# Three pairs of conditioning columns leave the first layer's attention steps

## The chip, the cores and the metric

One Trainium2 chip, of which the kernel uses one core. The metric is device time in microseconds for one execution. Before the change three runs took 1669.55, 1670.0 and 1672.5 us; their median, 1670.0 us, is the time before.

## The reference

Two encoder layers over 512 tokens of width 1024. With `c_act = silu(c)`, each layer computes its conditioning, mixes tokens, normalises, sends tokens through experts and normalises again:

```python
mod = c_act @ ada_w[i] + ada_b[i]                 # 6 * 1024 columns
sh1, sc1, g1, sh2, sc2, g2 = jnp.split(mod, 6)
h = x * (1 + sc1) + sh1
y = neighbourhood_mixer(h) if i == 0 else gqa_mixer(h)
x = layer_norm(ALPHA * x + (1 + g1) * y)
h = x * (1 + sc2) + sh2
y = hierarchical_moe(h)                           # 4 groups, 32 experts, top 2
x = layer_norm(ALPHA * x + (1 + g2) * y)
```

Everything is float32. So the six conditioning vectors of a layer are wanted at different times: `sh1, sc1` at its entry, `g1` after the mixer, `sh2, sc2` at the routing, `g2` in the experts. Each vector is two blocks of 512 columns, called (layer, block): blocks 0 and 1 are `sh1`, 2 and 3 `sc1`, 4 and 5 `g1`, 6 and 7 `sh2`, 8 and 9 `sc2`, 10 and 11 `g2`.

## The kernel before

**Conditioning.** A block needs 2 MB of weights, which come as two loads of 1 MB, (`ada`, layer, block, half). Blocks 0 to 3 of layer one are made at the very start. Seven others (`ADAV`) are accumulated on DVE, two multiply-adds in a step. Twelve (`ADAP`: six pairs and one single block) are made on PE by `adap`, in the steps of layer one's attention that `ADAP` names: for each block and half four matmuls, each with a 128x32 stationary operand (a shifted window of `Z`, which holds `c_act` in one column) and 512 moving columns, in four column groups of the array; a record of the trace is half of such a matmul, so a pair has 32. They add up in one PSUM tile, and a DVE add puts the sum into `mod[l]`, the SBUF tile in which every block has its row. `row` and `ada_cols` read it: `row` spreads a block over the partitions, `ada_cols` turns blocks into columns by four thin matmuls and one DVE operation for each vector.

**Layer one's attention** (`mixer0`, `neighbours`, `flow`) is 32 steps (16 heads in pairs, four blocks of queries). A step computes scores on PE, subtracts the maximum and adds the bias on DVE, exponentiates on ACT, turns the result on PE, copies it on ACT and multiplies by the values on PE. Between these, `flow` puts a fixed number of projection matmuls for later steps (`STREAM`, `RATE`), which last until about step 26. PE and DVE run in the order that is written here (`manual_schedule`).

**Layer one's output projection and routing** (`layer`, the block for `l == 0`): for each of four tiles of 128 tokens the projection (`sums`), the transposes (`turnX`), the router's logits, and two tiles later the `router`, a chain of small DVE operations with one PE step in the middle. PE's order is written out here as well. The last tile's transposes and logits follow behind that block, then `moe`, whose `begin` gathers the first experts' tokens while DVE routes the last tile.

**The experts** (`moe`): 32 experts by twos, 12 loads of 1 MB for each two, PE's order written out. At the end eight `unit`s close the sum over experts and DVE and ACT normalise (`scales`, `finish`). Then comes `overflow`, a block behind a branch that all engines take together.

**Layer two's mixer** (`mixer1`): it splits the key and value weights on ACT, DVE and POOL, turns X into eight transposed blocks on PE (PSUM tile `pt`, two buffers), scales them on ACT and DVE, and projects them; then four query projections, then `router_weights(1)`, which folds `sc2, sh2` into the router's weights. Here the order on all engines but SP is a planner's: it takes the earliest written instruction that its own estimate says is ready.

**Loads.** `plan` lists all weights in the order of their use; `W` hands one out, returns its slot to a list of free ones and issues the next loads of the list into free slots. All are issued by SP, in order, and each waits until its slot's last reader has finished, so one that waits holds up all behind it. Attention has 5 slots of 1 MB for such weights; the experts have 14 (5 of `w0`, 3 of `wy`, 2 of `no`, 4 of `nh`). Weights of layer two can only go into the 5 until layer two begins. In the stage of the output projection the list offers three `wy`, one `w0` and two `no`; the others are added behind it.

## Time and profile before

| | us |
|---|---|
| median of three runs | 1670.0 |
| profiled execution | 1673.3 |
| its span | 1671.6 |
| PE busy | 1574.7 (94%) |
| DVE busy | 700.6 (42%) |
| ACT busy | 437.6 (26%) |
| POOL busy | 162.3 (10%) |

The rows below come from that one execution. Times are us from the span's start unless marked ns. PE is the matrix engine, DVE the vector, ACT the scalar, POOL the general engine; SP issues the loads. A row of the timeline gives start, length, engine, line, operation, output and input tiles, shapes, the count of merged records, and in brackets how long the engine stood idle before it and what released it. Records overlap, so the length of a group is not its share of the engine: the pace is read from start to start.

### The profile page before, as it was taken

How to read it: one execution, taken by the hardware profiler on the slowest of the kernel's cores; microseconds unless marked ns; L12 is line 12 of the kernel's file. 1: busy time of each engine (PE TensorE's matmuls, PEld its weight loads, DVE VectorE, ACT ScalarE, POOL GpSimd, SP SyncE). 2: the span in 40 equal slices, each digit the busy share in tenths (PEclk: the TensorE clock that was granted, in tenths of full speed). 3: DMA queues.
4: the chain of work that ended last, by engine and by line, in shares of the span. 5: the costliest groups of instructions: out<-in, count | busy, mean ns of one | idle time of the engine just before them, and what ended most of it. 6: DMA issues, size and time to landing. Idle time of an engine off the chain costs nothing. (4 is left out here: it accounts for less than half of the span.)

```text
span 1671.6 us, 21362 instructions
## 1 busy us (share of the span) xinstructions
PE 1574.7 (94%) x8490; PEld 906.6 (54%) x8490; DVE 700.6 (42%) x1605; ACT 437.6 (26%) x934; POOL 162.3 (10%) x99
## 2 busy tenths in 40 slices
PE   7899997989999999999979989998999999999995
PEld 4676664773544545455448866766354545545442
DVE  3434545574232322323256865666432232323235
ACT  2343335231110111111134475453011111101112
POOL 2322212010000000000014250011000000000001
PEclk9999997999999999999989989999999999999997
DMA  9587872357999999999932000035899999999981
GB/s 328 196 309 269 331 306 104 137 202 295 417 419 420 419 419 420 419 419 420 420 125 102 26 1 25 1 125 206 368 416 420 420 420 420 419 420 420 419 332 51
DMA packets 76198, 493.17 MB, mean 295 GB/s; under 512 B 9876, under 2 KB 11284, under 8 KB 18876
## 3 DMA queue, kind: packets, MB, share of 16 engines
q1 hardware_dynamic: 71916, 485.05, 71.4%
q10 hardware_dynamic: 4176, 6.69, 1.2%
q8 instruction: 69, 1.13, 0.3%
q14 instruction: 37, 0.30, 0.1%
HBM read 489.61 MB, written 2.10 MB: 294 GB/s over the span
## 5 line engine op out<-in xcount | busy, mean ns | idle before, releaser
L300 PE MATMUL gu<-w,xT 128*64 128x512 f32 x2048 | 445.0, 592 | 0.0
L300 PEld LDWEIGHTS gu<-w,xT 128*64 128x64 f32 x2048 | 146.8, 137 | 291.6 <-issue 287.0
L300 PE MATMUL pd<-w,hx 128*64 128x512 f32 x1024 | 228.0, 598 | 0.0
L1391 DVE TENSOR_TENSOR h<-h,gu 128x512 f32<-128x512 f32 x32 | 22.0, 688 | 370.4 <-PE gu L300 370.4
L300 PEld LDWEIGHTS pd<-w,hx 128*64 128x64 f32 x1024 | 70.9, 137 | 140.3 <-issue 136.7
L300 PE MATMUL gc<-OH,zH 128*128 128x256 f32 x480 | 121.5, 291 | 2.6 <-DVE OH L1276 2.6
L300 PE MATMUL gc<-OH,zL 128*128 128x256 f32 x480 | 118.6, 284 | 0.0
L300 PE MATMUL gc<-YH,OT 128*128 128x512 f32 x244 | 104.2, 427 | 1.0 <-DVE X L1358 1.0
L1358 DVE TENSOR_TENSOR X<-X,gc 128x512 f32<-128x512 f32 x128 | 87.4, 688 | 39.3 <-PE gc L300 39.3
L300 PEld LDWEIGHTS gc<-OH,zH 128*128 128x128 f32 x480 | 92.5, 193 | 14.9 <-issue 11.4
L300 PE MATMUL gc<-YL,OT 128*128 128x512 f32 x244 | 96.3, 394 | 0.0
L300 PEld LDWEIGHTS gc<-OH,zL 128*128 128x128 f32 x480 | 92.6, 193 | 0.0
L300 PE MATMUL pw<-w,oH 128*128 128x512 f32 x256 | 86.3, 408 | 0.0
L1414 ACT ACTIVATE YH<-h 128x512 fp32r<-128x512 f32 x32 | 20.2, 630 | 233.6 <-DVE h L1413 233.6
L300 PE MATMUL pj<-wh,hTH 128*128 128x256 f32 (+1 forms) x272 | 71.2, 304 | 9.1 <-ACT hTH L419 4.0
L1294 ACT ACTIVATE xT<-gc,A 128x256 f32<-128x256 f32 x60 | 33.8, 566 | 173.9 <-PE gc L300 173.9
L300 PE MATMUL pj<-wl,hTH 128*128 128x256 f32 (+1 forms) x272 | 68.0, 292 | 0.0
L300 PE MATMUL pj<-wh,hTL 128*128 128x256 f32 (+1 forms) x272 | 65.6, 293 | 0.8 <-DVE hTL L427 0.8
L300 PEld LDWEIGHTS gc<-YH,OT 128*128 128x128 f32 x244 | 45.8, 188 | 37.3 <-DVE X L1358 15.8
L1292 DVE TENSOR_SCALAR xT<-gc,A 128x256 f32<-128x256 f32 x60 | 32.5, 545 | 76.9 <-ACT xT L1294 76.5
L1390 ACT ACTIVATE h<-gu 128x512 f32<-128x512 f32 x32 | 19.1, 597 | 173.0 <-PE gu L300 173.0
L303 PE MATMUL pt<-c_ident,pr 128*128 128x128 f32 x384 | 59.5, 283 | 2.1 <-ACT pr L862 2.0
(345 smaller groups left out, 2355.9 us busy)
## 6 DMA issues: line engine op xcount, KB each, us to landing
w<-in_gu SPq DMA_DIRECT2D x256, 1024.0 KB, 14.3
w<-in_dn SPq DMA_DIRECT2D x128, 1024.0 KB, 13.5
w<-in_ada SPq DMA_DIRECT2D x40, 1024.0 KB, 7.9
wq<-in_wqk SPq DMA_DIRECT2D x16, 512.0 KB, 3.6
w<-in_wo SPq DMA_DIRECT2D x8, 1024.0 KB, 5.8
w<-in_adaq SPq DMA_DIRECT2D x6, 1024.0 KB, 12.0
bias<-in_nab ACTq DMA_DIRECT2D x24, 256.0 KB, 3.4
w<-in_wq SPq DMA_DIRECT2D x4, 1024.0 KB, 4.9
```

What stands on the lines that cost most here:

```text
L300: return self.nc.tensor.matmul(out, l, r, start=start, stop=stop, **kw)
L303: self.nc.tensor.transpose(out, in_, self.ident)
L1292: nc.vector.tensor_scalar(xT[q][:, k, :], ps, s, b, op0=OP.mult, op1=OP.add)
L1294: nc.scalar.activation(xT[q][:, k, :], ps, AF.Identity, scale=s, bias=b)
L1358: nc.vector.tensor_tensor(X[t][:, c], X[t][:, c], ps, op=OP.add)
L1390: nc.scalar.activation(h, gu[0], AF.Silu)
L1391: nc.vector.tensor_tensor(h, h, gu[1], op=OP.mult)
L1414: nc.scalar.activation(YH[j][:, c], y, AF.Copy)
```

## The change

Of `ADAP`'s pairs, three go elsewhere. (0,10),(0,11), the gate `g2` of layer one (`ADAO`), is made at the end of the routing block of layer one, behind `router(NT - 2)`, in the PSUM tile `pw`; its four loads stand in the list ahead of the first expert weights. (1,6),(1,7), `sh2` of layer two (`ADAL[0]`), is made behind the last `unit` of layer one's experts, ahead of `scales` and `finish`; (1,8),(1,9), `sc2` of layer two (`ADAL[1]`), in `mixer1` behind the split of the first weights and ahead of the transposes. Their loads stand ahead of `kv` 0 and `kv` 1. The rest of `ADAP` moves from steps 4, 12, 23, 26 to 5, 11, 19, 26. The columns for `sc2` and `sh2` of layer two, which were made with those for `sc1` and `sh1` in the routing block of layer one, are made by a second `ada_cols` ahead of `router_weights(1)`.

```diff
--- before.py
+++ after.py
@@ -44,8 +44,8 @@
 QPOST = 2
 NWQ = 4
 ADAV = [(0, 6), (0, 7), (0, 8), (0, 9), (1, 0), (1, 1), (1, 2)]
-ADAP = {4: [(0, 4), (0, 5)], 8: [(0, 10), (0, 11)], 12: [(1, 4), (1, 5)], 15: [(1, 6), (1, 7)], 19: [(1, 8), (1, 9)],
-        23: [(1, 10), (1, 11)], 26: [(1, 3)]}
+ADAP = {5: [(0, 4), (0, 5)], 11: [(1, 4), (1, 5)], 19: [(1, 10), (1, 11)], 26: [(1, 3)]}
+ADAO, ADAL = [(0, 10), (0, 11)], [[(1, 6), (1, 7)], [(1, 8), (1, 9)]]
 STREAM = [("qk", 1, 0)] + [("qk", n, i) for i in (1, 2) for n in range(2)] + [("vq", 0)] \
     + [("qk", n, i) for i in (3, 4, 5, 6) for n in range(2)] + [("vq", 1)] + [("qk", n, 7) for n in range(2)]
 RATE = (18, 15)
@@ -133,6 +133,9 @@
         for l in range(DEPTH):
             if l:
                 for c in range(2):
+                    for z in ADAL[c]:
+                        for h in range(2):
+                            add(("ada", *z, h), a["ada"][z[0], z[1], h])
                     add(("kv", c), a["wkv1"][c])
                 for c in range(4):
                     add(("q1", c), a["wq1"][c])
@@ -142,6 +145,8 @@
             for h in range(2):
                 for kh in range(2):
                     add(("wl", l, h, kh), None)
+            if l == 0:
+                ada(0, *(j for _, j in ADAO))
             for j in range(E // 2):
                 for n in range(2):
                     for kh in range(2):
@@ -359,6 +364,18 @@
             nc.vector.tensor_scalar(dst[:, n].rearrange("p (j i) -> p j i", j=2),
                                     pc[:, :, j:j + 2].rearrange("p i j -> p j i"), one, None, op0=OP.add)
 
+    def ada_pair(self, pp, pair, tag):
+        l = pair[0][0]
+        ps = pp.tile([P, F], F32, name=tag, bufs=2)
+        for i, (_, j) in enumerate(pair):
+            for h in range(2):
+                w = self.W(("ada", l, j, h)).rearrange("p (k n) -> p k n", k=4)
+                for k in range(4):
+                    r = 32 * k
+                    self.mm(ps[r:r + 32], self.Z[:, 4 * h + k, 12 - j:44 - j], w[:, k, :], i == 0 and h == 0,
+                            i == len(pair) - 1 and h == 1, tile_position=(0, r))
+        self.nc.vector.tensor_tensor(self.mod[l], self.mod[l], ps, op=OP.add)
+
     def row(self, ps, l, j):
         return self.mm(ps, bcast(self.indc[:, j:j + 1], [P, P]), self.mod[l], True, True)
 
@@ -687,16 +704,7 @@
                 nc.vector.scalar_tensor_tensor(acc, w, s, acc, op0=OP.mult, op1=OP.add)
 
         def adap(pair):
-            l = pair[0][0]
-            ps = pp.tile([P, F], F32, name="pt")
-            for i, (_, j) in enumerate(pair):
-                for h in range(2):
-                    w = self.W(("ada", l, j, h)).rearrange("p (k n) -> p k n", k=4)
-                    for k in range(4):
-                        r = 32 * k
-                        self.mm(ps[r:r + 32], self.Z[:, 4 * h + k, 12 - j:44 - j], w[:, k, :], i == 0 and h == 0, i == len(pair) - 1 and h == 1,
-                                tile_position=(0, r))
-            nc.vector.tensor_tensor(self.mod[l], self.mod[l], ps, op=OP.add)
+            self.ada_pair(pp, pair, "pt")
 
         def aside(n):
             i, b = n // 4, n % 4
@@ -734,6 +742,7 @@
             self.fold_cols(c1[:, 0], c1[:, 1], self.lnc[:, 0, 2], self.lnc[:, 0, 3], self.col[1][:, 0], self.col[1][:, 1])
             w = self.W(("kv", 0))
             whl = [self.split(pool, w[:, 1024 * x:1024 * x + 1024], [P, 1024], 4, (nc.vector, None)[x]) for x in range(2)]
+            self.ada_pair(pp, ADAL[1], "pt")
             acc = [pp.tile([P, 4, HD], F32, name="pj", bufs=4) for t in range(NT)]
             for k in range(KD):
                 self.put_hT(k, self.transp(k, pp, "pt"), hH, hL, c1[:, 0], c1[:, 1], pool, k >= KACT)
@@ -841,6 +850,7 @@
                     if t == QPOST:
                         post()
                 post = lambda c=c, qq=qq, ss=ss: queries(c, qq, ss)
+            self.ada_cols(pp, self.mod[1], self.col[1], ((2, 8, 1.0), (3, 6, 0.0)), "pt")
             self.router_weights(1, pp)
             post()
 
@@ -1035,13 +1045,14 @@
                         if t:
                             hx = turnX(t - 1)
                         if t == NT - 1:
-                            self.ada_cols(pp, self.mod[1], self.col[1], ((0, 2, 1.0), (1, 0, 0.0), (2, 8, 1.0), (3, 6, 0.0)), "pt")
+                            self.ada_cols(pp, self.mod[1], self.col[1], ((0, 2, 1.0), (1, 0, 0.0)), "pt")
                         it = sums(t, 1)
                         run(it, 10)
                         if t:
                             logits(t - 1, lg[:, t - 1, :], hx)
                         run(it, 99)
                     self.router(NT - 2, wk, pp, "pt", lg[:, NT - 2, :], rt)
+                    self.ada_pair(pp, ADAO, "pw")
             else:
                 for t in range(NT):
                     oTs.append([wk.tile([P, KD, P], F32R, name=n, bufs=2) for n in ("oH", "oL")])
@@ -1490,6 +1501,8 @@
             seed(range(NSEED[0], 8))
             for n in range(8):
                 unit(n)
+            if l == 0:
+                self.ada_pair(pp, ADAL[0], "gc")
             self.scales(pool, rt, 0, NT)
             self.finish(l, units, acc, rt)
         self.overflow(l, zH, zL, G2, rt, OH)
```

## Rows read from the trace of the kernel before

**Rows 1.** The page: busy time by engine; DMA issues of one weight, us to landing.

```profile
PE 1574.7 (94%) x8490; PEld 906.6 (54%) x8490; DVE 700.6 (42%) x1605; ACT 437.6 (26%) x934; POOL 162.3 (10%) x99
...
w<-in_wq SPq DMA_DIRECT2D x4, 1024.0 KB, 4.9
```

**Rows 2.** Stretches: busy us (instructions) of each engine, granted clock, DMA share, GB/s.

```profile
95.00:258.00 163.00, 157.02 (x1046) 106.99 (x1044) 75.72 (x178) 60.31 (x151) 29.64 (x13) 0.98 0.78 297
...
360.20:367.00 6.80, 6.79 (x32) 6.80 (x33) 4.27 (x26) 2.88 (x6) 0.00 (x0) 0.50 0.58 245
...
395.00:405.00 10.00, 7.01 (x14) 2.04 (x14) 8.61 (x15) 0.00 (x0) 0.00 (x0) 0.66 0.70 291
...
405.00:415.00 10.00, 10.00 (x50) 3.24 (x48) 5.28 (x16) 1.26 (x2) 0.00 (x0) 1.00 0.68 272
...
800.00:810.00 10.00, 10.00 (x47) 4.00 (x44) 1.14 (x2) 0.60 (x1) 0.00 (x0) 1.00 1.01 419
...
861.50:867.80 6.30, 0.12 (x1) 0.00 (x0) 5.44 (x19) 4.92 (x10) 0.00 (x0) 0.81 0.00 1
...
867.80:879.00 11.20, 8.03 (x36) 7.66 (x37) 5.49 (x11) 7.35 (x9) 6.63 (x6) 0.50 0.16 41
```

**Rows 3.** PE in order of time, layer one's attention: start, us, instruction, idle before.

```profile
158.25 3.64 PE L300 MATMUL pt<-w,Z 128*32 128x512 f32 x32
...
161.83 0.66 PE L300 MATMUL po<-pts,V 128*64 128x128 f32 x8
...
177.75 2.78 PE L300 MATMUL pt<-w,Z 128*32 128x512 f32 x24
...
182.48 1.76 PE L300 MATMUL pt<-w,Z 128*32 128x512 f32 x8 [1.95 <-DMA w<-in_ada]
...
184.17 1.12 PE L300 MATMUL po<-pts,V 128*64 128x128 f32 x8
...
233.78 0.69 PE L300 MATMUL pj<-hTH,wh 128*128 128x512 f32 x1 [2.46 <-ACT V L479]
```

**Rows 4.** Tile pt in attention: ns of one, min/median/max.

```profile
L699 DVE TENSOR_TENSOR mod<-mod,pt x6: 686/689/690, 103.0 to 242.5; 128x512 f32<-128x512 f32 x6
...
L300 PE MATMUL pt<-c_indc,mod x8: 185/266/266, 226.2 to 226.9; 128*128 128x20 f32 x8
```

**Rows 5.** PE in order of time, layer one's last routing.

```profile
359.43 0.30 PE L303 MATMUL pt<-c_ident,X 128*128 128x128 f32 x1 [3.46 <-DVE Mb L1126]
...
360.21 3.63 PE L300 MATMUL pt<-c_wr,hx 128*128 128x36 f32 x16
...
372.27 0.36 PE L300 MATMUL gc<-OH,zH 128*128 128x256 f32 x1 [1.02 <-DVE OH L1276]
```

**Rows 6.** DVE in order of time, same stretch.

```profile
363.87 0.25 DVE L971 SCALAR_TENSOR_TENSOR lg3x<-cs,nm,pt 128x36 f32<-128x36 f32 x1 [2.22 <-PE pt L300]
...
371.70 0.42 DVE L1276 TENSOR_TENSOR OH<-c_iota,posx 128x256 fp32r<-128x256 f32 x1
```

**Rows 7.** SP's DMA issues: three moments, start, us, count.

```profile
289.39 2.01 SPq L272 DMA_DIRECT2D w<-in_gu  x4
...
850.86 3.76 SPq L272 DMA_DIRECT2D w<-in_wq  x2
...
877.85 0.34 SPq L272 DMA_DIRECT2D w<-in_wq  x1
```

**Rows 8.** PE in order of time, end of layer one and entry of layer two.

```profile
823.57 13.90 PE L300 MATMUL gu<-w,xT 128*64 128x512 f32 x64
...
867.85 1.94 PE L303 MATMUL pt<-c_ident,X 128*128 128x128 f32 x8 [6.23 <-ACTq L1169]
...
872.91 0.58 PE L300 MATMUL pj<-wh,hTH 128*128 128x256 f32 x1 [3.12 <-ACT hTH L419]
```

**Rows 9.** Weights' landing, issues of 800 to 808 us.

```profile
DMA to landing us min/median/max: 18.0/20.0/20.5
```

## The prediction

> **What bounds the kernel now.** I read the page's busy times first: PE is busy 94% of the span [rows 1], so the question of each stage is whether work on PE there stands alone or beside a wait. Then I cut the span into stages. In layer one's attention PE works 157.02 of 163.00 us at a granted clock of 0.98, while DVE has 75.72 and ACT 60.31 [rows 2]. The three pairs leave from there, and a matmul that goes there should give back nearly its own time. Then I read PE in order of time at the four places that receive something. At the last routing of layer one PE stands 3.46 us for DVE and afterwards works at half clock (0.50 from 360.2 to 367.0) [rows 2, 5]. At the end of layer one it stands 6.23 us at the branch ahead of the overflow block while DVE is busy 5.44 of 6.30 us [rows 2, 8]. At the entry of layer two it transposes, stands 3.12 us for ACT, and works at half clock until 879 [rows 2, 8]. In the expert blocks between, PE is busy 10.00 of 10 us and the DMA engines move 419 GB/s at a share of 1.01 [rows 2]: both are full, so loads that come late there are the thing to fear.
>
> **Attention: three pairs go.** A pair is 32 recorded matmuls. One that has its weights starts at 158.25 and the next work at 161.83: 3.58 us, with PE busy on both sides [rows 3]. Two of the three pairs are worth that, 7.16 us. The one at step 15 costs more. It starts at 177.75, stands 1.95 us for its fourth load, does its last 8 matmuls in 1.76 us, and the next work begins at 184.17: 6.42 us. That next work takes 1.12 us where it takes 0.66 elsewhere [rows 3], another 0.46. In sum 7.16 + 6.42 + 0.46 = 14.0 us. What is left has distances of 6, 8 and 7 steps between pairs instead of 3 or 4, and 12 MB fewer to load, so I expect no load to be late in its place. The 2.46 us wait for ACT at 231 [rows 3] hangs on the values' copies and stays. The shifted pairs (step 4 to 5, 12 to 11, 23's pair to 19) move equal work: nothing.
>
> **The last routing: one pair comes.** In PE's order, which is written out there, the pair stands behind the router's last matmul, which waits for DVE until 359.43; so it can't fill the 3.46 us. Behind it are the last transposes, the 16 logit matmuls and, through ACT, DVE's routing of the last tile: that chain runs from 363.87 to 372.12 [rows 6], and PE, which gathers meanwhile, is 1.02 us early for it [rows 5]. So the low end is 3.58 - 1.02 = 2.6 us. The high end is the whole pair at half clock, 7.2 us. I take 4.5: the pair's own 3.58 and a quarter of it at half clock (0.9), nearer to the low end because what follows at half clock today (3.63 us of logits [rows 5]) then finds less of that stretch left. DVE's add of the pair (0.69 [rows 4]) falls in DVE's 2.22 us wait for the logits [rows 6]: nothing. On the clock: the trace shows 0.50 after PE's stand, over a stretch whose first half is thin matmuls [rows 2, 5]. The Trainium skill (TensorE: Matmul & The Clock Gate, What's actually happening) says that the clock follows how busy PE has lately been; by that a dense pair would bring it back sooner and this term would come out near 3.6, a point less in the sum.
>
> The pair's four loads stand in SP's order ahead of the experts'. The four loads issued at 289.39 [rows 7] become the pair's; the experts' first two follow as today, and the third asks for the slot of the pair's first weight, which is free only at about 361. So 12 of the 14 slots fill after that: at 419 GB/s [rows 2] a load of 1.05 MB takes 2.5 us, 30 us in all, to 391. Each weight still lands ahead of its use: the last of the first expert pair's eight at 376 against a need after 390. What the lag of four loads (10 us) could do is drain the reserve later. But the DMA engines are idle 3.0 + 3.2 us between 395 and 415 [rows 2], so at most 3.8 us of it lasts. At the end of the stage the loads issued until 808 land 20.5 us later at most [rows 9], by 828.5, and the last of those weights is wanted three quarters into a 13.9 us block that starts at 823.57 [rows 8], at 834.0. The reserve of 5.5 us covers it: nothing, and 4.5 us if the idle time doesn't give any back.
>
> **The second norm: one pair comes.** Its loads take four slots that the next layer's first weights had; they are in by then, since the last two of today's loads into those slots are issued at 850.86 and up to 3.8 us later and land 4.9 us on [rows 1, 7]. PE does the pair in its idle 6.23 us. DVE is nearly full there, and its add of 0.69 sits among the normalisations that close the layer: 0.6 us. If DVE meets the add ahead of the scales it stands for the pair as well, at most 3.58 + 0.69 = 4.3. Below nothing: PE idles less and the 8.03 us of half-clock work behind [rows 2] could run faster; not all of that is on the path, I allow 2 us.
>
> **The entry of layer two: one pair comes.** Its loads wait for the slots of the pair before, so they are issued from about 862.3 to 865.0; the first lands 4.9 us later, at 867.2, and the fourth 7.5 us after that, at 874.7. The branch ends at 867.85. The pair asks for one of the two buffers that the transposes use and keeps it until its last matmul. Low end: half the pair and more fits in the 3.12 us wait [rows 8], 3.58 - 3.12 = 0.5. High end 10 us, worked out below as a rival. I take 3.0: the first two weights' matmuls in the wait (nothing), the last two behind it, 1.8 us at full and 3.6 at half clock, and a little for the buffer. Key weights of layer two now load at about 878 [the slot's release, rows 7], 5 us later they are in, about 11 us before they are wanted: nothing.
>
> **The shift columns.** Two of four columns are now made at the end of layer two's projections. The four matmuls at the old place stay; a second set of them comes: 8 records from 226.2 to 227.2 [rows 4], 1.0 us of PE. If it finds a gap it costs nothing, at half clock and in the chain of the router's weights 2.0; I take 0.8.
>
> **Sum.** -14.0 + 4.5 + 0.6 + 3.0 + 0.8 = -5.1 us. The profiled execution took 1673.3 us (its span of 1671.6 and 1.7 around it), 3.3 above the median of 1670.0; the terms don't depend on that, so 1668.2 in the one and 1664.9 us as the median.
>
> **Rivals.** (1) Slower: attention isn't PE's to give. If steps are paced by ACT and DVE (scores, exponent, turn, copy), the two pairs without a stall become waits of the same length, and only step 15's stall goes (6.42 - 3.58 + 0.46 = 3.3). Then -3.3 + 8.9 = +5.6: 1675.6. It decides once attention gives back less than the 8.9 us that the other places cost. For it speaks the wait on ACT [rows 3]; against it that PE idles only 6.0 of 163 us while neither other engine is half busy [rows 2]. Chance 0.12.
> (2) PE takes the pair at the entry ahead of the transposes and stands until its fourth weight, and the loads go out only behind the branch: 867.85 + 4.9 + 7.5 = 880.3, the last matmuls 0.9, transposes and ACT's first output 1.8, so 883.0 against 872.91 [rows 8]: 10 us, and -5.1 - 3.0 + 10 = +1.9: 1671.9. SP issued nothing between 854.6 and 877.85 [rows 7], which could be the branch; but nothing had a free slot then. Chance 0.16. The Trainium skill (DMA: Bandwidth & Descriptors, Issuing engines are not separate DMA queues) adds that ACT's loads of the rotary tables would share the same DMA engines with the pair's weights; no row here shows the two together, and by it POOL would start a little later.
> (3) The lag in the first experts is not given back: 10 - 5.5 = 4.5, and -0.6 in all: 1669.4. For it: both engines full for 400 us; against it: the idle time at 395 to 415. Chance 0.10.
> The forecast has 0.62.
>
> **How the numbers follow.** Within 0.2% (3.3 us) is what a measurement here can't tell from no change. The forecast's own range runs from -11 (pairs at the low ends, the entry in its wait) to +1 (the routing at 7.2, the entry at 6): 1659 to 1671. Of its 0.62, 0.52 is faster, 0.09 the same, 0.01 slower. Rival 1: 0.03 same, 0.09 slower. Rival 2: 0.01, 0.10, 0.05. Rival 3: 0.03, 0.06, 0.01. Faster 0.56, same 0.28, slower 0.16. The range for 8 in 10 runs from 1658 to 1673.5; it leaves out most of rival 1 and the forecast's lowest corner.
>
> **What would show it.** Right: attention ends some 14 us earlier with no wait for ada loads; the pair stands behind the router's last matmul and the first expert block starts 4 to 5 us later against the end of attention; PE works in the idle time ahead of the branch; no PE wait for loads in the experts; the first projection of layer two starts 2 to 4 us later against the branch. Wrong: new waits on ACT or DVE in attention (rival 1), a wait for ada at the entry (rival 2), waits for expert weights near 830 (rival 3). I am most unsure of the planner's order on PE at the entry.

## The result and the profile after

In five rounds on one chip the kernel before took 1671.9 us (median) and the changed one 1681.6: ratio 1.0065 (95% interval 1.0044 to 1.0086), slower by 0.65%: 9.7 us between the medians, 10.9 by the ratio of the paired rounds. The forecast was 5 us faster; the measured median lies 8 us above the range. The profiled execution of the changed kernel took 1679.05 us with a span of 1677.3, 5.7 above the span before, and is the fastest of its five, while that of before was 3.3 us above its median. That gap comes back below.

The busy times don't show it: PE is busy as long as in [rows 1].

```profile
PE 1576.6 (94%) x8498; PEld 905.5 (54%) x8498; DVE 702.3 (42%) x1605; ACT 437.3 (26%) x934; POOL 161.4 (10%) x99
```

So I cut both spans at the same rows of PE's timeline: the first matmul of the layer's gate `g1` (`pw<-mod`), the first `trib` matmul of a router, the first expert matmul (`gu`), the first `unit` (`gc<-YH`), the first row behind the branch (its exit), the first key transpose (`kd`) and the layer's first scores (`ps<-kHH,w`). The lengths in us, and what the prediction put there:

| stretch | before | after | difference | predicted |
|---|---|---|---|---|
| start to g1 (attention) | 293.2 | 281.3 | -11.9 | -14.0 |
| g1 to first router matmul | 34.1 | 33.9 | -0.2 | 0 |
| to first expert matmul (last routing) | 49.4 | 54.7 | +5.2 | +4.5 |
| to first unit (experts) | 480.6 | 480.8 | +0.2 | 0 |
| to the branch's exit (second norm) | 10.5 | 12.6 | +2.1 | +0.6 |
| to the key transposes (entry) | 48.0 | 55.4 | +7.4 | +3.0 |
| to the scores (with the columns) | 65.7 | 71.0 | +5.3 | +0.8 |
| the rest | 690.0 | 687.6 | -2.4 | 0 |
| sum | 1671.6 | 1677.3 | +5.7 | -5.1 |

The experts and the rest move from one execution to the next in kernels that differ in nothing there: in the runs below the experts take 478.0 to 480.8 us and the rest 687.6 to 691.9. So -2.4 is no effect.

The stretches of the changed kernel that answer to [rows 2] (columns as there): attention at full clock as before, the last routing at 0.72, the end of layer one and the entry with the DMA engines at a share of 0.82 to 0.84 where they were at 0.00 and 0.16, and the end of the projections at 0.67.

```profile
90.00:250.00 160.00, 151.77 (x997) 109.43 (x996) 75.36 (x184) 64.45 (x157) 30.86 (x13) 0.99 0.63 232
...
348.90:355.00 6.10, 6.10 (x41) 2.03 (x40) 3.31 (x15) 0.65 (x4) 0.00 (x0) 0.72 0.52 169
...
856.00:863.20 7.20, 2.50 (x24) 0.52 (x16) 5.24 (x20) 3.73 (x8) 0.00 (x0) 0.85 0.84 323
863.20:880.00 16.80, 13.79 (x88) 7.37 (x88) 4.80 (x6) 8.06 (x10) 0.55 (x1) 0.86 0.82 325
...
966.00:992.00 26.00, 21.78 (x111) 18.40 (x109) 12.50 (x56) 12.08 (x31) 3.44 (x3) 0.67 0.00 1
```

PE in order of time, the same kernel, to be read against [rows 3, 5, 8]. In attention two waits are new, 1.77 us for ACT ahead of the pair at step 5 and 1.40 for DVE at step 12. The gate's pair stands behind the router's matmul and takes 5.34 us, where a pair at full clock takes 3.64; the logits behind it are twice as fast as before (1.93 us against 3.63 in [rows 5]). The second norm's pair follows the units at once. At the entry PE takes its pair ahead of the transposes and stands for the third and fourth weight; the first projection then comes 9.5 us behind the exit instead of 5.1, and 12 and 21 us later PE waits for POOL and DVE. The last three rows are the columns and the two router matmul groups that hang on them.

```profile
103.87 0.73 PE L305 MATMUL pj<-wh,hTH 128*128 128x256 f32 x4 [1.77 <-ACT qk L627]
...
107.11 3.64 PE L305 MATMUL pt<-w,Z 128*32 128x512 f32 x32
...
160.82 0.66 PE L305 MATMUL po<-pts,V 128*64 128x128 f32 x8 [1.40 <-DVE w L903]
...
348.75 0.30 PE L308 MATMUL pt<-c_ident,X 128*128 128x128 f32 x1 [3.46 <-DVE Mb L1137]
...
348.99 5.34 PE L305 MATMUL pw<-w,Z 128*32 128x512 f32 x32
...
354.64 1.93 PE L305 MATMUL pt<-c_wr,hx 128*128 128x36 f32 x16
...
854.86 3.64 PE L305 MATMUL gc<-w,Z 128*32 128x512 f32 x32
863.28 3.65 PE L305 MATMUL pt<-w,Z 128*32 128x512 f32 x16 [4.78 <-PEq L1180]
867.48 1.26 PE L305 MATMUL pt<-w,Z 128*32 128x512 f32 x8 [0.55 <-DMA w<-in_ada]
870.24 1.06 PE L305 MATMUL pt<-w,Z 128*32 128x512 f32 x8 [1.50 <-DMA w<-in_ada]
871.23 0.66 PE L308 MATMUL pt<-c_ident,X 128*128 128x128 f32 x4
...
872.76 0.39 PE L305 MATMUL pj<-wh,hTH 128*128 128x256 f32 x1
...
884.52 0.39 PE L305 MATMUL pj<-wl,hTH 128*128 128x256 f32 x1 [2.06 <-POOL wl L318]
...
893.65 0.74 PE L305 MATMUL pj<-wh,hTL 128*128 128x256 f32 x4 [2.10 <-DVE hTL L444]
...
970.98 0.96 PE L305 MATMUL pt<-c_indc,mod 128*128 128x20 f32 x8
973.97 3.60 PE L305 MATMUL pt<-c_wr,A 128*128 128x36 f32 x16 [2.02 <-DVE rtt L289]
978.31 3.60 PE L305 MATMUL pt<-c_wr,Zo 128*128 128x36 f32 x16 [0.74 <-DVE rtu L297]
```

The other engines of the changed kernel around the branch: DVE's add of the pair waits for PE and sits ahead of `rsx`, on which all normalisations hang; ACT issues the rotary and gain tables 1.9 us behind the exit; POOL's first work with them starts 16.2 us behind it. SP sends the value weights 2.1 us behind the exit and four query weights behind them, two at 867.5 and 870.3, two at 884.5 and 884.9.

```profile
858.57 0.69 DVE L377 TENSOR_TENSOR mod<-mod,gc 128x512 f32<-128x512 f32 x1 [0.29 <-PE gc L305]
...
865.15 0.34 ACTq L733 DMA_DIRECT2D rt<-in_rope  x1
865.60 2.63 ACTq L736 DMA_DIRECT2D kk<-in_gain  x4
...
879.45 2.72 POOL L738 TENSOR_TENSOR rt<-rt,kk 128x256 f32<-128x256 f32 x3 [517.36 <-PE pt L308]
...
865.41 0.34 SPq L277 DMA_DIRECT2D w<-in_wkv  x1
867.51 17.79 SPq L277 DMA_DIRECT2D w<-in_wq  x4
```

In the kernel before, POOL starts 4.4 us behind the exit at 867.85:

```profile
872.29 2.75 POOL L730 TENSOR_TENSOR rt<-rt,kk 128x256 f32<-128x256 f32 x3 [502.33 <-DMA kk<-in_gain]
```

The gains' landing (the DMA view, 845 to 885 us: count, KB each, median us from issue to landing), before:

```profile
kk<-in_gain ACTq DMA_DIRECT2D x4, 32.0 KB, 2.9
```

and in the changed kernel:

```profile
kk<-in_gain ACTq DMA_DIRECT2D x4, 32.0 KB, 11.0
```

### The profile page after: what moved, and what is told of

Same layout as the page of the kernel before. It is cut to its first block, busy times and chain, and to the rows that moved or that the text cites. A ratio compares the mean times of both kernels' runs of the same rounds, so it can differ in the third digit from the quotient of the medians.

```text
span 1677.3 us, 21374 instructions
## 1 busy us (share of the span) xinstructions
PE 1576.6 (94%) x8498; PEld 905.5 (54%) x8498; DVE 702.3 (42%) x1605; ACT 437.3 (26%) x934; POOL 161.4 (10%) x99
## 5 line engine op out<-in xcount | busy, mean ns | idle before, releaser
L305 PEld LDWEIGHTS gc<-OH,zH 128*128 128x128 f32 x480 | 92.3, 192 | 14.7 <-issue 11.4
L305 PE MATMUL pj<-wh,hTH 128*128 128x256 f32 (+1 forms) x272 | 70.5, 302 | 7.5 <-ACT wh L317 2.8
```

The lines of the kernel that those rows point to most:

```text
L305: return self.nc.tensor.matmul(out, l, r, start=start, stop=stop, **kw)
```

## The experiments

Each ran in five rounds beside the kernel before; its trace is cut at the rows of the table above (us). The ratio comes from all executions, the stretches from one, and that one can lie far from its kernel's median (e9's took 1670.0 us against 1662.7, e3's 1675.7 against 1682.8). Kernels with the same attention differ by up to 5 us to g1 (e10 and e13), and kernels with the entry of the changed one by 2.4 (e11 and e15). So a difference of 2 or 3 us in a column stands on the waits behind it, not on the length alone.

| run | ratio to before | to g1 | last routing | norm | entry | to scores |
|---|---|---|---|---|---|---|
| before | | 293.2 | 49.4 | 10.5 | 48.0 | 65.7 |
| changed | 1.0065 [1.0044, 1.0086] | 281.3 | 54.7 | 12.6 | 55.4 | 71.0 |
| e12 columns late | 1.0034 [1.0024, 1.0044] | 289.4 | 49.4 | 10.5 | 48.2 | 70.5 |
| e1 columns early | 1.0034 [1.0022, 1.0047] | 282.2 | 52.5 | 12.4 | 58.0 | 62.3 |
| e4 without the pairs | 0.9977 [0.9963, 0.9992] | 285.6 | 49.5 | 10.5 | 48.4 | 68.1 |
| e5 old steps | 1.0057 [1.0037, 1.0077] | 279.0 | 54.7 | 12.4 | 55.8 | 70.8 |
| e2 pair behind | 1.0053 [1.0035, 1.0070] | 282.7 | 52.5 | 12.4 | 52.1 | 70.3 |
| e3 loads only | 1.0080 [1.0064, 1.0095] | 282.0 | 52.5 | 12.4 | 55.7 | 70.5 |
| e7 tables first | 1.0056 [1.0038, 1.0073] | 282.3 | 52.5 | 12.4 | 51.5 | 71.0 |
| e6 pair behind, loads held | 1.0029 [1.0018, 1.0041] | 281.9 | 54.0 | 12.1 | 48.5 | 70.3 |
| e11 add written behind | 1.0077 [1.0060, 1.0093] | 282.8 | 52.5 | 12.3 | 55.3 | 71.0 |
| e18 add last | 1.0077 [1.0055, 1.0099] | 285.9 | 54.4 | 12.3 | 57.7 | 70.4 |
| e15 gate pair first | 1.0083 [1.0057, 1.0109] | 282.1 | 52.0 | 12.3 | 57.7 | 70.4 |
| e10 all mends | 1.0043 [1.0029, 1.0058] | 277.4 | 54.7 | 12.4 | 63.5 | 60.9 |
| e13 columns in the middle | 0.9999 [0.9984, 1.0015] | 282.6 | 54.0 | 12.3 | 49.7 | 71.0 |
| e8 one pair | 0.9976 [0.9963, 0.9990] | 287.0 | 49.5 | 11.4 | 53.5 | 60.9 |
| e14 pair twice | 1.0007 [0.9991, 1.0023] | 288.2 | 51.0 | 12.8 | 52.5 | 61.2 |
| e9 one pair, tuned | 0.9961 [0.9948, 0.9974] | 290.0 | 51.0 | 11.4 | 49.5 | 61.9 |
| e16 two pairs | 0.9983 [0.9970, 0.9997] | 282.8 | 52.0 | 11.4 | 52.8 | 60.6 |
| e17 one pair, add last | 0.9956 [0.9938, 0.9974] | 289.5 | 51.0 | 11.1 | 47.3 | 61.4 |

**All three out.** `ADAO` and `ADAL` with their loads dropped.

> The changed kernel with the three moved pairs left out altogether, loads included (g2 of layer one, sh2 and sc2 of layer two are left out); the second ada_cols stays. By the terms read from the two traces the three places cost 5.2 + 2.1 + 7.7 = 15.0: 1666.6, ratio 0.991; attention unchanged against the changed kernel, which makes it 11.5 us shorter than before. By the terms of the prediction the places cost 4.5 + 0.6 + 3.0 = 8.1: 1673.5, ratio 0.995, and what is lost would have to lie elsewhere, in attention or the columns.

Against the changed kernel 1.0065 - 0.9977 = 0.88%, 14.7 us, give or take 4: the three places cost more than 8.1. Routing, norm and entry are back at the values of before to 0.4 us. The run to g1 is 4 us longer than in the changed kernel with the same attention; there ACT waited longer for its load at step 5 and PE 3.31 us for ACT.

**Attention: the steps.**

```diff
-ADAP = {5: [(0, 4), (0, 5)], 11: [(1, 4), (1, 5)], 19: [(1, 10), (1, 11)], 26: [(1, 3)]}
+ADAP = {4: [(0, 4), (0, 5)], 12: [(1, 4), (1, 5)], 23: [(1, 10), (1, 11)], 26: [(1, 3)]}
```

> The changed kernel with the four entries left in attention at the steps they had before (4, 12, 23, 26 instead of 5, 11, 19, 26). Theory A: at step 4 the pair was work for PE while ACT waited for a load of query and key weights; one step later PE meets that wait bare (1.77 us in the trace of the changed kernel, 3.31 us and half clock behind it in one other), and the step 12 one meets a DVE wait of 1.40 us in the same way. Then attention ends 2 to 4 us earlier, the sum of the three removed pairs comes to the 14.0 of the prediction, ratio to the changed kernel 0.998. Theory B: equal work costs the same at any of these steps, 0 us, ratio 1.000, and the 11.5 us are what the three pairs were worth.

To g1 it is 2.3 us shorter, and both new waits are gone (PE waits 0.45 us for ACT behind step 4's pair). The wait at step 5 is one for a load: in the changed kernel ACT stands for query and key weights there.

```profile
101.30 1.06 ACT L317 ACTIVATE wh<-wq 128x1024 fp32r<-128x1024 f32 x1 [3.61 <-DMA wq<-in_wqk]
```

In e5 ACT idles 4.98 us at the same instruction while PE does the pair. All ten kernels with the shifted steps have PE's wait at step 5 (1.77 to 3.31 us), the three with the old steps (e5, e10, e13) have 0.45 in its place; that much of theory A is shown. Its size is not: to g1 the ten take 281.3 to 285.9 us (median 282.3), the three 277.4, 279.0 and 282.6, and the ratios 1.0057 and 1.0065 can't be told apart. Its 14.0 doesn't hold, as the next runs show.

**Columns.** e12 is the kernel before with only its columns late; e1 the changed kernel with them early.

```diff
-            self.ada_cols(pp, self.mod[1], self.col[1], ((2, 8, 1.0), (3, 6, 0.0)), "pt")
-            self.router_weights(1, pp)
             post()
...
                 nc.scalar.activation(V[:, t, :], ps, AF.Copy)
+            self.ada_cols(pp, self.mod[1], self.col[1], ((2, 8, 1.0), (3, 6, 0.0)), "pt")
+            self.router_weights(1, pp)
             post = keys
```

> The kernel before, all pairs at their places, but the columns of sc2 and sh2 of layer two made by a second ada_cols ahead of router_weights(1), as in the change. The prediction's term: +0.8 (0 to 2.0), ratio 1.0005. By the trace of the changed kernel (the end of the mixer slips by 5.3 us behind its middle) and that without the three pairs (2.7 us): +2.7 to +5.3, ratio 1.0016 to 1.003, with c_wr,A waiting some 2 us for DVE's chain.

> The changed kernel with the second ada_cols and router_weights(1) written behind the value projection instead of behind the four query projections; PE then does them among the transposes and the value projection of layer two. Theory A (the columns at the end stand in a chain PE, DVE, PE, DVE, PE that nothing covers there): the 4.7 us by which the end of the mixer slips go away, 1681.6 - 4.7 = 1677, ratio to the changed kernel 0.997; the two 3.6 us groups c_wr,A and c_wr,Zo no longer stand at 974 to 982. Theory B (it is only a stretch at half clock, which would come there with any work): 0 to -1.5 us, ratio 0.999 to 1.000.

Moving the columns alone costs 0.34%, 5.7 us; the stretch to the scores is 4.8 us longer. Two rows of e12's PE timeline: the pair of step 15, and the router group that now waits for DVE and takes 3.60 us. From the transposes ahead of the router groups to those behind them it takes 12.7 us, as in the changed kernel, and 8.0 before. Written early they give it back: 71.0 to 62.3 us, and the ratio falls from 1.0065 to 1.0034. (The entry of e1 is 2.6 us longer than the changed kernel's; e15 and e18, which have the columns late, are as long.)

```profile
177.40 3.93 PE L300 MATMUL pt<-w,Z 128*32 128x512 f32 x32
...
967.21 3.60 PE L300 MATMUL pt<-c_wr,A 128*128 128x36 f32 x16 [2.03 <-DVE rtt L284]
```

In the kernel before, DVE had folded the columns at the entry, 100 us ahead of the same group, which then waits for nothing and takes half the time:

```profile
868.23 0.17 DVE L408 TENSOR_TENSOR A<-A,col 128x8 f32<-128x8 f32 x1
...
967.91 1.87 PE L300 MATMUL pt<-c_wr,A 128*128 128x36 f32 x16
```

The first row of e12 settles another point. e12 has the attention of before, and the pair at step 15 does not wait for its fourth load here: the wait of 1.95 us and the slow rows behind it in [rows 3] belong to that one execution. To g1 e12 takes 289.4 us, 3.8 less than the profiled execution of before, which was 3.3 above its median (e12's was 1.5 below its own). Against e12 three pairs at the old steps give back 10.4 us in e5, 12.0 in e10 and 6.8 in e13, around 3 x 3.58 = 10.7; the changed kernel gives back 8.1, and the ten with its steps 7.2 in the median. Whole times say the same: e4 and e12 both have late columns and differ by the three pairs, and 1.0034 - 0.9977 is 0.57%, 9.5 us, give or take 3. For the pair of step 15 alone the traces show little: the four kernels with only that one moved take 287.0 to 290.0 us to g1.

**The entry.** e2 writes the pair behind the transposes and the key projection, e3 keeps its loads and drops its matmuls, e7 issues the tables by SP ahead of the value weights, e6 is e2 with the four loads held until SP is through the branch.

```diff
# e2
-            self.ada_pair(pp, ADAL[1], "pt")
             acc = [pp.tile([P, 4, HD], F32, name="pj", bufs=4) for t in range(NT)]
...
+            self.ada_pair(pp, ADAL[1], "pt")
             def proj(key):
# e7
-            nc.scalar.dma_start(rt[:, 0:2], a["rope"])
+            nc.sync.dma_start(rt[:, 0:2], a["rope"])
# e6, in W, ahead of the norm's pair, and ahead of kv 0
-        while self.wi < len(self.wl):
+        while self.wi < min(self.lim, len(self.wl)):
+                self.lim = self.wpos["ada", 1, 8, 0]
+            self.lim = 1 << 30
```

> The changed kernel with the four loads of sc2 of layer two at their place, but without the pair's matmuls and its DVE add (sc2 is left out of layer two's columns). Theory A (the pair on PE makes the entry late): about -7 us, 1674.5, ratio 0.9957, with POOL's first multiply at the tables 4.4 us behind the branch's exit as in the kernel before. Theory B (the loads make it late): POOL still starts some 16 us behind the exit and the entry stays within 2 us of that of the changed kernel: 1680, ratio 0.999.

> The changed kernel with the pair sc2 of layer two written behind the eight transposes and the key projection instead of ahead of them. Theory A (PE takes the pair first and the transposes stand behind its loads): the transposes start at the branch's exit again, the key projection ends 4 to 7 us earlier against the branch, the pair then costs its own 3.6: 1681.6 - 4 = 1677.5, ratio 0.9976. Theory B (the loads of the pair delay the rotary and gain tables, so POOL's halves of the split key weights come late whatever PE's order): POOL's first multiply with the tables still starts 15 to 16 us behind the branch's exit, PE still waits for wl and hTL, 0 to -2 us, ratio 0.999 to 1.000.

> The changed kernel with the loads of the rotary and gain tables issued by SP ahead of the value weights instead of by ACT. Theory A (the value and first query weights, whose slots are now free at the entry, fill the DMA engines ahead of these small loads): the gains land in 3 to 5 us instead of 11, POOL's first multiply starts 6 to 9 us behind the branch's exit instead of 16, PE's waits for wl and hTL shrink by 3 to 4 us; ratio to the changed kernel 0.998. Theory B (POOL is late because PE's pair holds it up): POOL starts 16 us behind the exit again, 0 us.

> The kernel of the run with sc2's pair behind the transposes, and in addition its four loads held back until the entry of layer two, so that none is under way at the branch ahead of the overflow block. Theory A (loads under way slow the way through the branch and the first table loads behind it): PE leaves the branch 0.2 us behind DVE's and ACT's last work instead of 1.4, ACT issues the table loads within 0.1 us of that instead of 1.9, the first projection starts 5 us behind the exit instead of 8; in all 3 to 4 us less than with the pair behind alone, ratio to before 1.003, unless the pair's weights then come late. Theory B (the pair on PE and DVE makes the exit late): the exit stays where it is, 0 us, ratio to before 1.0053.

Without a single matmul of the pair the entry takes 55.7 us, as with it: in e3 the transposes start at the exit, 859.99, and yet POOL starts 18.2 us behind it, when the gains land (12.4 us from issue).

```profile
878.20 2.20 POOL L738 TENSOR_TENSOR rt<-rt,kk 128x256 f32<-128x256 f32 x3 [516.65 <-DMA kk<-in_gain]
```

With the tables ahead of the freed slots' loads the gains land in 5.1 us, POOL starts its table work 8.4 us behind the exit and the entry shrinks by 3.9 us (e7); with the pair behind, so that its slots stay taken and nothing follows the tables at once, the gains land in 5.2 us and the entry shrinks by 3.3 (e2). These stretches and their waits are what shows it: the whole times of e2, e3 and e7 can't be told from the changed kernel's. With the four loads held back as well, the pair inside, the entry takes 48.5 against 48.0 before (e6), 3.6 less than e2: all but 0.5 of the pair's 3.6 us is hidden, and the ratio is 1.0029. ACT there issues the tables ahead of PE's exit, the gains land in 4.9 us, and POOL starts 6.1 us behind the exit:

```profile
862.55 1.94 PE L309 MATMUL pt<-c_ident,X 128*128 128x128 f32 x8 [4.25 <-PEq L1182]
```

```profile
862.38 0.34 ACTq L734 DMA_DIRECT2D rt<-in_rope  x1
```

So about half of the price of the entry is what slots set free let through: the value weights and two of the four query weights, issued from 865.4 to 870.3, share the 16 DMA engines with the last of the pair's own loads and with the small table loads, which then hold POOL's halves of the key weights. The Trainium skill (DMA: Bandwidth & Descriptors, Issuing engines are not separate DMA queues) says that loads of different issuers interleave on the same engines; 11.0 us against 2.9 agree. The other half goes with the four loads ahead of the branch: SP itself stood 5.2 us at the branch (L1180) in the changed kernel, and in the kernels with three pairs whose four loads went out ahead of the branch the tables' first load came 1.8 to 2.2 us behind PE's exit, by ACT or by SP; in e6, where SP passes first, it came 0.2 ahead. Why stays open: in e8, with one pair, four loads go out ahead of the branch and SP stands there 4.6 us, and yet the tables' first load comes at PE's exit. What is left in e7, 3.5 us above before, can be PE's own wait for the pair, since its first projection comes 10.9 us behind the exit; no run shows it alone.

**The norm.** e11 writes the add behind `finish`; e18 (and e17, on e9) writes DVE's order out as well; e14 does the pair's matmuls twice.

```diff
-                self.ada_pair(pp, ADAL[0], "gc")
-            self.scales(pool, rt, 0, NT)
-            self.finish(l, units, acc, rt)
+                add = self.ada_pair(pp, ADAL[0], "gc", True)
+                with tc.manual_schedule(engines={mybir.EngineType.DVE}):
+                    self.scales(pool, rt, 0, NT)
+                    self.finish(l, units, acc, rt)
+                    add()
```

> The changed kernel with the DVE add of the norm's pair written behind finish. From the first unit to the branch's exit it takes 10.5 us before and 12.6 after. Theory A (the add and its wait of 0.29 in the chain of scales are all): back to 10.6, -2 us, ratio to the changed kernel 0.9988. Theory B (0.98 are the add, the other 1.1 come at the branch itself): 11.6, -1 us, ratio 0.9994. The time is too near to the noise for either; the stretch in the trace decides.

> The kernel with only sh2 of layer two moved, its matmuls done twice (the second set into a PSUM tile that nothing reads). From the first unit to the branch's exit: 10.53 us without a pair, 11.39 with it. Theory A (PE needs 3.5 us or more of its own to get through the branch, so only 6.2 - 3.5 = 2.7 us of its idle time could hide a pair): the second set shows in full, 11.39 + 3.6 = 15.0 us, in all +3.6 us, ratio to before 0.9997. Theory B (the 0.9 us is the DVE add in the chain of scales, PE has time to spare): 6.2 us of idle time less 3.6 leave 2.6, so the second set shows with 1 us, or with the 3.6 by which the add then waits longer and no more: 12.4 us if the add's input is the first set's.

> The changed kernel with the add behind the last normalisation in the same way. There PE leaves the branch 1.1 to 1.4 us behind DVE's and ACT's last work, by its own queue. If that lag follows DVE and ACT: from the first unit to the exit 12.5 - 1 = 11.5 us, ratio to the changed kernel 0.9994. If PE's queue is late by itself (its exit lies 4.5 us behind the end of the pair whatever the others do): 12.4, as before, and DVE's and ACT's last work lies 2 us ahead of the exit. The time can't tell them apart, the stretch can.

e11 tells nothing: the planner left the add where it was (ahead of `rsx`), so it is the changed kernel once more, and its 1.0077 repeats that kernel's 1.0065. e18 does move it, and the exit stays at 12.3 us: DVE's add ends at 865.8 and ACT's work at 865.2, PE leaves at 867.18, by its own queue.

```profile
859.05 3.64 PE L305 MATMUL gc<-w,Z 128*32 128x512 f32 x32
867.18 3.65 PE L305 MATMUL pt<-w,Z 128*32 128x512 f32 x16 [4.49 <-PEq L1183]
```

Doubling the pair refutes the theory that PE always needs 3.5 us for the branch: in e14 it is out 1.4 us behind its last matmul. (e14 as a whole is 0.31%, 5 us, slower than e8, the same kernel without the second set; 1.4 us of that lie in this stretch, the rest is not placed.)

```profile
857.83 7.14 PE L304 MATMUL gc<-w,Z 128*32 128x512 f32 x64
866.38 1.07 PE L307 MATMUL pt<-c_ident,X 128*128 128x128 f32 x8 [1.41 <-DVEq L1181]
```

With one pair moved (e8) the norm takes 11.4 us; PE leaves 0.14 us behind ACT's last work, as before, and the add in DVE's chain, with its wait, is of the size of the 0.9. With the add last it takes 11.1 (e17), since the exit then follows the add. In the kernels with three pairs 1 us more comes from PE's queue, 4.2 to 4.8 us behind the pair whatever DVE does. Why it is late there stays open. All twelve of them load a 16 KB packet of instructions there, and PE's exit comes 2.7 to 2.8 us behind its start in every one; the kernels with one pair load such a packet too, from 4.5 us ahead of the exit to 0.2 behind it, so it doesn't set them apart. The Trainium skill (Runtime: NRT & Kernel Launch, Instruction fetch mechanics) says that a taken branch can force a fetch of instructions by DMA; no run here tests it.

**The last routing.** The pair written ahead of `router(NT - 2)`.

> The changed kernel with the gate's pair ahead of router(NT - 2) instead of behind it, so that PE can do it in the 3.46 us in which it waits for DVE there. From the first router matmul of the stage to the first expert matmul it takes 49.4 us without the pair, and 52.5 or 54.7 with it. Theory A (the pair now lies in the wait): 49.5, -3 us or -5, ratio to the changed kernel 0.997 to 0.998. Theory B (the wait only moves, because the router's matmul then waits for the pair and DVE's chain hangs on that): 52 to 53, 0 to -1 us.

It does fill the wait (348.36, 0.31 us left), but the second half of the transposes then stands 2.42 us for DVE, and the logits take 3.21 us where they took 1.93. 52.0 us, where the changed kernel and its kin take 52.5 to 54.7 and kernels without the pair 49.4 to 51.0: theory B.

```profile
344.26 3.64 PE L305 MATMUL pw<-w,Z 128*32 128x512 f32 x32
...
348.36 0.18 PE L305 MATMUL pt<-Mb,trib 128*128 128x32 bf16 x1 [0.31 <-DVE Mb L1137]
...
351.44 0.66 PE L308 MATMUL pt<-c_ident,X 128*128 128x128 f32 x4 [2.42 <-DVE posx L1141]
```

The column of the table mixes two things here. From the third tile's logits to the first expert matmul it takes 26.5 us in all seven kernels without the pair, 29.6 in seven with it, 30.3 in three (the changed kernel among them), 28.9 in e18, and 29.1 with the pair ahead of the router: the pair costs 2.4 to 3.8 us. The other 1.4 to 2.5 us of the longer columns lie at the first router step, ahead of the pair, and come in kernels without it too (e9, e14, e17). Before and after:

```profile
350.22 1.87 PE L300 MATMUL pt<-c_wr,hx 128*128 128x36 f32 x16
...
376.75 1.51 PE L300 MATMUL gu<-w,xT 128*64 128x512 f32 x6
```

```profile
339.54 1.87 PE L305 MATMUL pt<-c_wr,hx 128*128 128x36 f32 x16
...
369.84 1.98 PE L305 MATMUL gu<-w,xT 128*64 128x512 f32 x4
```

**Together.** e10 joins the mends of attention, entry and columns (its add stayed ahead of `rsx`, as in e11); e13 moves its columns behind the second query projection. e8 is the kernel before with only step 15's pair moved, to the norm, and the columns early; e9 holds its loads back and lets SP load the tables first; e16 moves the gate's pair of e9 ahead of the router as well; e17 adds the written DVE order.

> The changed kernel with all its mends: the attention steps as before (4, 12, 23, 26), the norm's add behind finish, sc2's pair behind the transposes with its loads held back until the entry, the columns and router_weights(1) behind the value projection. All three pairs stay moved. By the terms: attention -14.2, last routing +3.5, norm +1, entry +4 (the pair's own 3.6 and little more), the columns 0: -5.7 against before, 1664.3, ratio 0.9966. If the places share one limit (loads at the entry, the clock) so that the mends don't add up: within 2 us of before, ratio 0.999 to 1.001.

> The kernel with all mends, but the columns and router_weights(1) behind the second query projection instead of behind the value projection. In the kernel with all mends they stood between a late sc2 and the key transposes: from the branch's exit to the layer's first scores it took 124.4 us, against 118.7 with the columns at the end. Theory A (the mends do add up, only the columns stood in front of their own input): the stretch comes to 114 (118.7 less the 4.9 that the late columns cost alone), the attention stays 14 us shorter, 1676.4 - 10 = 1666, ratio to before 0.998. Theory B (the places share one limit): the stretch stays over 120, ratio 1.003.

> The kernel before, with only the pair of attention step 15 moved (sh2 of layer two, to the second norm), and the columns of sc2 and sh2 with router_weights(1) written behind the value projection. By the terms measured so far: attention -6.9 (the pair with its stall for the fourth load), the norm +2.0, the tables behind the loads of four freed slots 0 to +4, the columns 0: in all -5 to -1, ratio to before 0.997 to 0.9995. By the rival that attention's stall only moves to the next pair (its loads come late there instead): -1.6 + 2 and so no gain, ratio 1.000.

> The kernel with only sh2 of layer two moved (to the second norm), with three edits: the DVE add of that pair written behind finish, the loads behind kv 0 held back until the entry of layer two, and the tables' loads issued by SP ahead of them. If the price of the norm is the add (0.98 us) and the price of the entry is the four loads that freed slots let through ahead of the tables (5 us more from the branch's exit to the first key transposes than in the kernel before, some 2.5 of them the columns that now stand there), it gains 1 + 2.5 = 3.5 us on the kernel with one pair moved: 1664.6 - 3.5 = 1661, ratio to before 0.9955. If the entry's extra is the columns' alone, only the 1 us comes: ratio 0.997.

> The fastest kernel so far (sh2 moved to the second norm, add behind finish, loads held back, tables first: 1662.7 us, ratio to before 0.9961) with the gate's pair moved as well, from attention step 8 to the place ahead of router(NT - 2). If that place is free and a pair in attention is worth 3.6: 1659, ratio 0.994. If the place costs 3 us as the one behind the router does: 1662, ratio 0.9958, no gain.

> The fastest kernel so far (e9), with DVE's order written out from scales to the add, so that the add really stands behind the last normalisation (in e9 and e11 the planner left it ahead of rsx, and the edit changed nothing). From the first unit to the branch's exit e9 takes 11.37 us, the kernels without a pair there 10.53. If the add in the chain is the whole price: 10.6, -0.8 us, 1661.9, ratio to before 0.9956. If the way through the branch then ends with the add (0.7 us at its end): 11.2 to 11.4, no gain.

e10's 1.0043 missed both of its forecasts. With the columns early its entry takes 63.5 us: they hang on `sc2`, which the pair behind makes late. In the middle that is gone, but the stretch to the scores is long again (71.0). From the exit to the scores e13 takes 120.7 us, as its second theory has it; its time lies between the two, and three moved pairs with their mends end where the kernel before does (0.9999). One pair does better: e9 0.9961 and e17 0.9956, 6.5 and 7.4 us faster than before, the best of all and not to be told apart. How much of that is the pair is not shown: to g1 they take 290.0 and 289.5 us, no less than e12, while the entry and the stretch to the scores take 108.7 us in e17 and 113.7 before. No run has early columns and tables with all pairs at their old steps. The gate's pair as a second one loses 0.2% again (e16 against e9, give or take as much).

## Why the prediction was wrong

By stretches the change costs in its own trace: attention -8.1 (against e12), last routing +3.8 at the pair's place, norm +2.1, entry +7.4, columns +5.3 (4.8 in e12), so 10.5 us in all, where 9.7 to 10.9 were measured. That it comes so near is partly luck: in other traces with the same stage attention gives back as little as 3.5, and the entry costs up to 9.7.

- **Attention, -14.0.** It gave back 8.1. That PE bounds it was right in the main: about 3 x 3.58 came back at the old steps. The 3.3 us for step 15's stall were read from one execution and are not there in e12; booking them, and "the terms don't depend on that", was the step that failed. That they are the same 3.3 us by which this execution lay above its median is likely but not shown. And "the shifted pairs move equal work: nothing" failed: at step 4 the pair covered ACT's wait for a load, at step 5 PE meets it, 1.77 us (2.3 from e5 to the changed kernel).
- **Last routing, +4.5.** The place was right, the size some 1.5 too high: 3.0 in most kernels, 3.8 in this trace. The pair pays 1.7 us for a lower clock and the logits behind it get 1.7 back, as the second reading in the prediction had it (near 3.6).
- **Experts, 0.** Right: no load was late (rival 3).
- **Norm, +0.6.** It cost 2.1. DVE met the add ahead of `rsx`, as feared (0.9 to 1.0); PE's own queue at the branch was not thought of (1).
- **Entry, +3.0.** It cost 7.4. PE's order was that of rival 2, yet its loads went out ahead of the branch, and e3 shows that PE's wait did not set the length. "Key weights of layer two now load at about 878 ...: nothing" failed: freed slots let the value weights out at 865.4 and two query weights behind them, onto engines that the tables needed (3.3 to 3.9 us), and the tables themselves were issued 1.9 us late behind the loads ahead of the branch (3.6 from e2 to e6). The prediction named a meeting of tables and loads, that with the pair's own, and gave it no price.
- **Columns, +0.8.** I priced the second set of matmuls and allowed 2.0 for the chain. It cost 4.8 (e12), because the chain matmul, DVE column, fold, router group, which before had its fold done 100 us early, now runs at a place where nothing covers it: PE waits 2.03 us for DVE, and both router groups take 3.60 us, the granted clock of the stretch being 0.67.

Rival 1 had the right sign by the wrong cause: attention did give back 7 to 10 us, and the other places cost twice what was booked.

## What to carry to other kernels

Before a stall of one profiled execution is booked as a gain, look for it in a second execution of the same stage. Work that leaves a full stage must be priced where it lands by its whole chain: the loads that its freed slots let through, the small loads they meet, and the consumers that used to find their input ready. Two moments can be equal in work and not in cover: look what the moved piece was hiding.

## What the runs showed of the hardware

Four loads of 32 KB land 2.9 us behind their issue in the kernel before, 5.2 with the last two of four 1 MB loads still under way (e2), and 11.0 with three more of 1 MB issued around them (the changed kernel; 12.4 in e3, with four more). PE's way out of the branch ahead of the overflow block took 1.4 us behind its last matmul in one program (e14) and 4.2 to 4.8 in the twelve with three pairs. Sixteen logit matmuls take 3.63 us at a granted clock of 0.50 behind PE's stand, and 1.93 at 1.00 behind the pair (the lower level and the full one).
